# A decoder layer on one core: dense steps between the state-space matmuls, and the embedding's result staged in the tiles of later operands

## The chip, the cores and the metric

The kernel runs on 1 core of one Trainium2 chip. The metric is the device time of one execution in microseconds (us); lower is better. Several executions are timed and the median is quoted; one execution more is profiled.

## What is computed

One layer of a decoder trunk in float32, with 1024 tokens of 1024 channels. Four token mixers of 256 channels each run on the same stream, and a gated sum of their outputs goes through one projection. A squared-ReLU MLP and a gated embedding follow. Cut to what matters here:

```python
proj = h @ w_in[i]
(s5_u, fq, fk, fv, ff, rw, sq, sk, sv, gates) = _split(proj, IN_SPLIT_SIZES)
y_s5 = _s5_mixer(s5_u, ...)          # diagonal complex state space, 16 groups of 16 channels
y_fox, y_rwkv, y_sb = ...            # forgetting attention, RWKV-7, stick-breaking attention
merged = sum(jax.nn.sigmoid(gates[:, :, n]) * (branches[n] @ w_branch[i, n])
             for n in range(N_BRANCHES))
h = _layer_norm(DEEPNORM_ALPHA * h + merged @ w_out[i], ln1_g[i], ln1_b[i])
ffn = jnp.square(jax.nn.relu(h @ mlp_w1[i])) @ mlp_w2[i]
ple = jax.nn.sigmoid(h @ ple_gate_w[i]) * (p[i] @ ple_w[i])
h = _layer_norm(DEEPNORM_ALPHA * h + ffn + ple, ln2_g[i], ln2_b[i])
```

Inside `_s5_mixer` a scan over the tokens gives the states, `y` is the output of the states and of the input, and then `y = gelu(y)` and `y * sigmoid(y @ glu_w + glu_b)`.

## The kernel before, in words

Nearly all dense products are made of three matmuls of 128x512 each, because both operands are split into a high and a low part (high by high, high by low, low by high). The function `dense` makes such a product; it yields after each step of 128 rows of the contraction, that is after three matmuls. In the first part of the kernel, the projections, weights are `wh` and `wl` (or `vh` and `vl` for the branches' up-projections) and the operands are the tiles `t` (the input x) and `y` (a mixer's output). Weights come in as `wr`, ScalarE casts them to `wh` and VectorE makes `wl`.

The mixers are written as generators, run by a planner (the class `Driver`). It keeps a clock of its own, made of estimated costs. `run(fill, until)` goes on with the generator that is due and has the best priority; when none is due it takes one step from `fill`, the dense projections. A generator that says `yield None` is due again 0.2 us of planned time later, so that one dense step is taken before it goes on; a number sets another time. The order that comes out is binding for TensorE, VectorE and ScalarE. The DMA queues of SP and POOL are ordered by the tile scheduler. Since every instruction of VectorE, ScalarE and the queues is issued by a wrapper (`Timed`), most of them stand at line 280; matmuls stand at line 327 and transposes at 332.

The state-space mixer has two generators. `s5_tables` makes matrices from the parameters: eight pairs of matmuls of `Gm` by `bd` go into a tile `lo`, and `Gm` is transposed in 16 pieces, four to a PSUM tile, which ScalarE copies to `GT`. Then `s5` runs twice, over 8 groups of channels each: 16 matmuls of `GT` by `U` give the inputs of the states, VectorE rotates them, scans over the tokens and rotates back (`X`), and an output loop makes for each of 8 groups one matmul of `Tg` by `U` and two of `Hm` by `X`. A GELU follows. When both passes are done, `gw` by `yt` makes the gate, in 128x512 float32. The result `ynat` is stored to `scr_Y` in DRAM, and loaded back as `wr`, to be split to the operand `y` of the up-projection. The next mixer, the stick-breaking attention, loads `raw` and `st` (keys, queries and values), multiplies `KH`, `KL` by `QS`, makes `R` and `W` on ScalarE, scans on VectorE, and transposes `W`.

The MLP is computed with a scheme that combines blocks of weights and operands before multiplying (seven products take the place of eight). Before it, `ple_half` makes the embedding's product, eight tiles for each half of the tokens; each is evicted from PSUM by ScalarE with a factor of 0.5 and stored to `scr_B`. Once the pool `sp` is open, the eviction takes a tile from `sn()`: ten buffers with a live count that the planner watches, shared with the intermediate results of the MLP's operand combinations. The operands of the first four products lie in other tiles; those of the last ones (`T3`, `B22`, `T4`) are [128, 1024] tiles with the tag `sx`, 12 buffers. Weight combinations are made partly by DMAs of POOL that accumulate (`wr<-wl`, `wl<-wr`), and `wp` are the split weight pairs.

Lines that the change touches: 1331 (`lo`), 1343 (transposes of `Gm`), 1424 (output loop of `s5`) and 2086 to 2092 (`ple_half`).

Of the kernel before, what the change touches and what calls it, by code (L numbers as in the profile page):

```python
# [9 lines left out]
F32 = mybir.dt.float32  # L10
# [6 lines left out]
P = 128  # L17
# [299 lines left out]
def body(ctx, tc, I, O, dbg=None):  # L317
# [25 lines left out]
    def nm(s):  # L343
        uid[0] += 1
        return f"{s}_{uid[0]}"
# [924 lines left out]
    def s5_tables(pool):  # L1270
        pw, fr, fi = s5v["pw"], s5v["fr"], s5v["fi"]

        def small(shape, name):
            return pool.tile(shape, F32, tag="s2k", name=nm(name), bufs=4)
        bc_in = small([P, 4, 8, 16], "bcin")
        SY.dma_start(out=bc_in, in_=I["s5_bc"])
        br, bi, cr, ci = (bc_in[:, i] for i in range(4))
        dsb = small([P, 256], "dsb")
        G.dma_start(out=dsb, in_=I["s5_d"].partition_broadcast(P))
        zz = small([112, 256], "zz")  # L1280
        G.memset(zz, 0.0)
        SY.dma_start(out=SCR["L"][128:240], in_=zz)

        def t1k(shape=(P, 8, 8, 16)):
            return pool.tile(list(shape), F32, tag="t1k", name=nm("t1k"), bufs=2)
        E = pool.tile([P, 2, P, 8], F32, tag="E", name="E", bufs=1)
        V.memset(E[:, 0, 0, :], 1.0)
        V.memset(E[:, 1, 0, :], 0.0)

        def grow(k):  # L1290
            n = 1 << k
            bcs = [x.unsqueeze(1).to_broadcast([P, n, 8]) for x in s5v["steps"][k]]
            cmul(E[:, 0, n:2 * n, :], E[:, 1, n:2 * n, :], E[:, 0, 0:n, :], E[:, 1, 0:n, :], bcs[0], bcs[1],
                 lambda: t1k((P, 64, 8))[:, :n, :])

        def b16(a):
            return a.unsqueeze(2).to_broadcast([P, 8, 16])
        bb = pool.tile([P, 2, 8, 16], F32, tag="bb", name="bb", bufs=1)

        def t128():  # L1300
            return pool.tile([P, 8, 16], F32, tag="t128", name=nm("t128"), bufs=4)
        for k in range(5):
            grow(k)
            if k % 2:
                yield 0.1
        cmul(bb[:, 0], bb[:, 1], b16(fr), b16(fi), br, bi, t128)
        nci = pool.tile([P, 8, 16], F32, tag="nci", name="nci", bufs=1)
        ts(nci, ci, -1.0, ALU.mult)
        bd = pool.tile([P, 2, 8, 2, 16], F32, tag="bd", name="bd", bufs=1)
        G.memset(bd, 0.0)  # L1310
        for e in range(2):
            es = slice(e * 64, e * 64 + 64)
            for i, w in ((0, cr), (1, nci)):
                A.copy(bd[es, i, :, e, :], w[es])
        yield 0.1
        pwp = pw.rearrange("p i j a -> p i a j")
        Gm = pool.tile([P, 2, 8, 8, 16], F32, tag="a", name="Gm", bufs=1)
        Hm = pool.tile([P, 2, 8, 8, 16], F32, tag="Hm", name="Hm", bufs=1)

        def bj(a):  # L1320
            return a.unsqueeze(3).to_broadcast([P, 8, 8, 16])

        def bh(a):
            return a.unsqueeze(2).to_broadcast([P, 8, 8, 16])
        prev = [pwp[:, i, :, 7::-1] for i in range(2)]
        pnx = [pwp[:, i, :, 1:9] for i in range(2)]
        cmul(Gm[:, 0], Gm[:, 1], bj(prev[0]), bj(prev[1]), bh(bb[:, 0]), bh(bb[:, 1]), t1k)
        yield 0.1
        lo = px()
        for pr in range(8):  # L1330
            for i in range(2):
                T.matmul(lo[:, pr * 32:pr * 32 + 32], lhsT=Gm[:, i, pr].rearrange("p s h -> p (s h)"),
                         rhs=bd[:, i, pr].rearrange("p e h -> p (e h)"), start=i == 0, stop=i == 1)
        Ls = small([P, 256], "Ls")
        tt(Ls.rearrange("p (g h) -> p g h", h=16), dsb.rearrange("p (g h) -> p g h", h=16),
           cc("eye7").unsqueeze(1).to_broadcast([P, 16, 16]), ALU.mult)
        tt(Ls, Ls, lo[:, 0:256], ALU.add)
        SY.dma_start(out=SCR["L"][0:128], in_=Ls)
        GT = pool.tile([P, 2, 8, P], F32, tag="GT", name="GT", bufs=1)
        for i in range(2):  # L1340
            for p4 in range(2):
                o = px()
                for j in range(4):
                    T.transpose(o[:, j * P:(j + 1) * P], Gm[:, i, p4 * 4 + j].rearrange("p s h -> p (s h)"), ident)
                A.copy(GT[:, i, p4 * 4:p4 * 4 + 4, :].rearrange("p a b -> p (a b)"), o)
        U = pool.tile([P, 16, P], F32, tag="a", name="U", bufs=1)
        for s in range(8):
            SY.dma_start(out=U[s * 16:(s + 1) * 16], in_=SCR["u"].rearrange("(g h) s c -> s h g c", h=16)[s])
        a1, a2 = t1k(), t1k()
        tt(a1, bj(pnx[0]), bh(cr), ALU.mult)  # L1350
        tt(a2, bj(pnx[1]), bh(ci), ALU.mult)
        tt(Hm[:, 0], a1, a2, ALU.subtract)
        yield 0.1
        a1, a2 = t1k(), t1k()
        tt(a1, bj(pnx[0]), bh(nci), ALU.mult)
        tt(a2, bj(pnx[1]), bh(cr), ALU.mult)
        tt(Hm[:, 1], a1, a2, ALU.subtract)
        Tg = pool.tile([P, 16, 8, 16], F32, tag="Tg", name="Tg", bufs=1)
        for s in range(0, 8, 2):
            Tz = small([P, 2, 256], "Tz")  # L1360
            for i in range(2):
                SY.dma_start(out=Tz[:, i, :], in_=SCR["L"][(7 - s - i) * 16:(7 - s - i) * 16 + 128])
            A.copy(Tg[:, :, s:s + 2, :], Tz.rearrange("p s (g h) -> p g s h", h=16))
        for k in range(5, 7):
            grow(k)
            yield 0.1
        yield from s5(pool, GT, Tg.rearrange("p g s h -> p g (s h)"), Hm.rearrange("p i a s h -> p i a (s h)"),
                      E.rearrange("p i j a -> p i a j"), U)

    def s5(pool, GT_, Tg_, Hm_, E_, U_):  # L1370
# [9 lines left out]
        for p4 in range(2):  # L1380
# [37 lines left out]
            for g4 in range(2):  # L1418
                o = px()
                for j in range(4):  # L1420
                    g = j * 2 + g4
                    pr, es = g // 2, slice((g % 2) * 64, (g % 2) * 64 + 64)
                    os_ = o[:, j * P:(j + 1) * P]
                    T.matmul(os_, lhsT=Tg[:, g], rhs=U[:, g, :], start=True, stop=False)
                    for i in range(2):
                        T.matmul(os_, lhsT=Hm[es, i, pr], rhs=X[es, i, pr, :], start=False, stop=i == 1)
                w = pool.tile([P, 512], F32, tag="s2k", name=nm("gl"), bufs=4)
                A.activation(out=w, in_=o, func=AF.Square)
                V.tensor_scalar(out=w, in0=w, scalar1=0.044715, scalar2=1.0, op0=ALU.mult, op1=ALU.add)
                tt(w, o, w, ALU.mult)  # L1430
                A.activation(out=w, in_=w, func=AF.Tanh, scale=math.sqrt(2.0 / math.pi))
                V.scalar_tensor_tensor(out=Ye[:, g4], in0=w.rearrange("p (a b) -> p a b", b=P), scalar=1.0,
                                       in1=o.rearrange("p (a b) -> p a b", b=P), op0=ALU.add, op1=ALU.mult)
# [87 lines left out]
    def sp():  # L1521
        return late["sp"]
# [272 lines left out]
    def sn():  # L1795
        live["sn"] += 1
        return sp().tile([P, 512], F32, tag="sn", name=nm("sn"), bufs=NSN)

    def drop(what):
        live[what] -= 1  # L1800
# [268 lines left out]
    def ple_half(h):  # L2069
        for dt_ in range(8):  # L2070
            k = 2 + dt_ // 2
            while (h, k) not in fed_units:
                yield "wait"
            o = pmm()
            for kt in range(2):
                xa, xb = fed_units[h, kt]
                ks = slice(dt_ % 2 * 256 + kt * P, dt_ % 2 * 256 + kt * P + P)
                a, b = (x[:, ks] for x in fed_units[h, k])
                T.matmul(o, lhsT=a, rhs=xa, start=kt == 0, stop=False)
                T.matmul(o, lhsT=a, rhs=xb, start=False, stop=False)  # L2080
                T.matmul(o, lhsT=b, rhs=xa, start=False, stop=kt == 1)
                yield
            if dt_ % 2:
                used_units.add((h, k))
            here = "sp" in late
            t = sn() if here else tpool.tile([P, 512], F32, tag="th", name=nm("pb"), bufs=2)
            A.activation(out=t, in_=o, func=AF.Copy, scale=0.5)
            SY.dma_start(out=SCR["B"][dt_][:, h * 512:(h + 1) * 512], in_=t)
            if here:
                drop("sn")  # L2090

    def open_sp():
        while tdone[0] < 8:
# [158 lines left out]
```

## Time and profile before

| what | value |
|---|---|
| median of 3 runs | 1868.21 us |
| lowest and highest | 1867.77 and 1874.67 us |
| profiled execution, its own time | 1875.13 us |
| its span, first to last instruction | 1873.3 us |
| mean granted clock of TensorE | 0.983 |
| busy share of TensorE, VectorE, ScalarE, GpSimd | 97%, 66%, 38%, 11% |
| mean DMA rate | 147 GB/s |

The span is cut to stretches by views of the trace, which give for each engine its busy time and for TensorE the granted clock (1.00 is 2.4 GHz, 0.50 is 1.2 GHz). A timeline gives start and length of each instruction or run of like instructions and, in brackets, the idle time before it and what ended that. Starts of successive matmuls are a better measure of their rate than lengths, since matmuls overlap.

### The profile page before, as it was taken

The page shows a single profiled execution, that of the slowest core. Times are in us where ns is not written, and L with a number is a line of the kernel's source. Part 1 is how long each engine was busy: PE and PEld are TensorE (multiplying, and loading weights), DVE is VectorE, ACT ScalarE, POOL GpSimd, SP SyncE. Part 2 cuts the span into 40 slices and gives each one's busy share as a digit, 9 for nine tenths or more (in the row PEclk, how much of TensorE's full clock was granted, in tenths as well). Part 3 has the DMA queues.
Part 4 walks back from the last instruction along what each step waited for, and adds up shares of the span by engine and source line. Part 5 has one row for each costly group of instructions (what it writes and reads, how often), then busy time and mean ns, then how long its engine had stood idle before and what let it go on. Part 6 is the DMA issues. An engine that isn't in the chain of part 4 may idle for free. (4 is left out here: it accounts for less than half of the span.)

```text
span 1873.3 us, 27588 instructions
## 1 busy us (share of the span) xinstructions
PE 1816.4 (97%) x9651; PEld 1479.0 (79%) x9651; DVE 1237.8 (66%) x2596; ACT 714.3 (38%) x1412; POOL 206.9 (11%) x279
## 2 busy tenths in 40 slices
PE   8999999998999999999999998999999999999998
PEld 6877777777788877777877886788888887888876
DVE  7675855616876765688867667666656565866574
ACT  5443343215554212555544125343333343433230
POOL 0331111100000000000000001111121111111000
PEclk9999999999999988999999999999999999999999
DMA  7334223124422411412155118898989898988441
GB/s 254 108 123 112 76 81 95 63 69 139 146 90 78 104 38 50 137 54 67 44 197 160 62 57 234 239 254 223 255 235 251 212 268 256 284 212 229 127 147 48
DMA packets 178012, 275.27 MB, mean 147 GB/s; under 512 B 37824, under 2 KB 59616, under 8 KB 177744
## 3 DMA queue, kind: packets, MB, share of 16 engines
q1 hardware_dynamic: 155552, 226.31, 37.3%
q0 software_dynamic: 22320, 47.18, 12.8%
q8 instruction: 76, 1.25, 0.3%
q14 instruction: 64, 0.52, 0.1%
HBM read 199.76 MB, written 56.89 MB: 137 GB/s over the span
## 5 line engine op out<-in xcount | busy, mean ns | idle before, releaser
L327 PE MATMUL mm<-t,wh 128*128 128x512 f32 x1600 | 514.3, 403 | 3.8 <-ACT th L280 1.9
L327 PEld LDWEIGHTS mm<-t,wh 128*128 128x128 f32 x1600 | 293.8, 190 | 66.5 <-issue 2.4
L327 PE MATMUL mm<-t,wl 128*128 128x512 f32 x800 | 314.9, 394 | 0.0
L327 PE MATMUL x<-t,wp 128*128 128x512 f32 x1152 | 270.8, 394 | 14.1 <-DVE wp L280 6.8
L327 PEld LDWEIGHTS x<-t,wp 128*128 128x128 f32 x1152 | 217.7, 190 | 64.3 <-DVE wp L280 9.9
L327 PE MATMUL x<-sx,wp 128*128 128x512 f32 x768 | 179.6, 389 | 0.2 <-DVE wp L280 0.2
L327 PEld LDWEIGHTS mm<-t,wl 128*128 128x128 f32 x800 | 151.8, 190 | 33.4
L327 PEld LDWEIGHTS x<-sx,wp 128*128 128x128 f32 x768 | 144.1, 188 | 30.5 <-DVE wp L280 0.7
L280 ACT CAST wh<-wr 128x512 fp32r<-128x512 f32 (+1 forms) x125 | 74.5, 596 | 123.1 <-PE mm L327 90.7
L280 DVE TENSOR_TENSOR wp<-wr,wp 128x512 fp32r<-128x512 f32 x96 | 65.8, 687 | 77.2 <-ACT wp L280 77.2
L280 ACT CAST wp<-wr 128x512 fp32r<-128x512 f32 x96 | 59.1, 620 | 147.8 <-DMA wr<-wl 69.3
L280 POOL TENSOR_TENSOR wl<-wr,wh 128x512 fp32r<-128x512 f32 x50 | 67.7, 1353 | 280.6 <-ACT wh L280 280.4
L327 PE MATMUL mm<-t,wp 128*128 128x512 f32 x384 | 90.6, 392 | 0.0
L327 PE MATMUL mm<-sx,wp 128*128 128x512 f32 x384 | 89.6, 389 | 0.0
L327 PE MATMUL mm<-wo,t 128*128 128x512 f32 x384 | 89.0, 391 | 0.0
L327 PEld LDWEIGHTS mm<-t,wp 128*128 128x128 f32 x384 | 72.6, 189 | 15.6 <-DVE wp L280 0.4
L327 PEld LDWEIGHTS mm<-sx,wp 128*128 128x128 f32 x384 | 72.1, 188 | 14.9
L327 PEld LDWEIGHTS mm<-wo,t 128*128 128x128 f32 x384 | 71.6, 188 | 14.5
L280 DVE TENSOR_TENSOR wl<-wr,wh 128x512 fp32r<-128x512 f32 (+1 forms) x75 | 47.3, 633 | 40.4 <-ACT wh L280 39.5
L280 DVE TENSOR_TENSOR wp<-wl,wp 128x512 fp32r<-128x512 f32 x64 | 43.7, 687 | 42.5 <-ACT wp L280 42.5
L280 DVE TENSOR_TENSOR wp<-wh,wp 128x512 fp32r<-128x512 f32 x64 | 43.9, 689 | 33.7 <-ACT wp L280 33.7
L280 ACT CAST wp<-wl 128x512 fp32r<-128x512 f32 x64 | 39.3, 620 | 50.0 <-DMA wl<-wr 16.5
(380 smaller groups left out, 3199.4 us busy)
## 6 DMA issues: line engine op xcount, KB each, us to landing
wr<-in_w_in_dram SPq DMA_DIRECT2D x110, 256.0 KB
scr_H<-sn SPq DMA_DIRECT2D x100, 256.0 KB
wr<-in_mlp_w_dram SPq DMA_DIRECT2D x84, 256.0 KB
sn<-scr_H SPq DMA_DIRECT2D x84, 256.0 KB
wh<-in_mlp_w_dram SPq DMA_DIRECT2D x56, 256.0 KB
wl<-in_mlp_w_dram SPq DMA_DIRECT2D x56, 256.0 KB
wr<-wl POOLq DMA_DIRECT2D x32, 256.0 KB, 6.5
wl<-wr POOLq DMA_DIRECT2D x32, 256.0 KB, 4.7
```

What stands on the lines that cost most here:

```text
L280: r = f(*a, **kw)
L327: return nc.tensor.matmul(out, lhsT=lhsT, rhs=rhs, **kw)
```

## The change

Three `yield None` are put into the state-space mixer: after each of the 8 pairs of `lo`, after each of the 4 groups of transposes, and after each of the 16 groups of the output loop (8 in each pass). Between these the planner now takes a dense step. And the evictions of `ple_half` take the first half of an `sx` tile once the pool is open, in place of a tile from `sn()`; the live count no longer holds them.

```diff
             for i in range(2):
                 T.matmul(lo[:, pr * 32:pr * 32 + 32], lhsT=Gm[:, i, pr].rearrange("p s h -> p (s h)"),
                          rhs=bd[:, i, pr].rearrange("p e h -> p (e h)"), start=i == 0, stop=i == 1)
+            yield None
...
                 for j in range(4):
                     T.transpose(o[:, j * P:(j + 1) * P], Gm[:, i, p4 * 4 + j].rearrange("p s h -> p (s h)"), ident)
                 A.copy(GT[:, i, p4 * 4:p4 * 4 + 4, :].rearrange("p a b -> p (a b)"), o)
+                yield None
...
                     T.matmul(os_, lhsT=Tg[:, g], rhs=U[:, g, :], start=True, stop=False)
                     for i in range(2):
                         T.matmul(os_, lhsT=Hm[es, i, pr], rhs=X[es, i, pr, :], start=False, stop=i == 1)
+                    yield None
...
             here = "sp" in late
-            t = sn() if here else tpool.tile([P, 512], F32, tag="th", name=nm("pb"), bufs=2)
+            t = (sp().tile([P, 1024], F32, tag="sx", name=nm("pb"), bufs=12)[:, 0:512] if here else
+                 tpool.tile([P, 512], F32, tag="th", name=nm("pb"), bufs=2))
             A.activation(out=t, in_=o, func=AF.Copy, scale=0.5)
             SY.dma_start(out=SCR["B"][dt_][:, h * 512:(h + 1) * 512], in_=t)
-            if here:
-                drop("sn")
```

TensorE, output loop of the state-space mixer, before (second half of the first pass; `x_` is the output's PSUM tile, `mm_` that of a dense product):

```order
L327 MATMUL x_7490<-U,Tg 128x128
L327 MATMUL x_7490<-X_7310,Hm 128x128 x2
L327 MATMUL x_7490<-U,Tg 128x128
L327 MATMUL x_7490<-X_7310,Hm 128x128 x2
L327 MATMUL x_7490<-U,Tg 128x128
L327 MATMUL x_7490<-X_7310,Hm 128x128 x2
L327 MATMUL x_7490<-U,Tg 128x128
L327 MATMUL x_7490<-X_7310,Hm 128x128 x2
L327 MATMUL mm_7464<-t_111,wh_7317 128x512
L327 MATMUL mm_7464<-t_110,wh_7317 128x512
L327 MATMUL mm_7464<-t_111,wl_7318 128x512
```

The same place after the change:

```order
L327 MATMUL x_7342<-U,Tg 128x128
L327 MATMUL x_7342<-X_7174,Hm 128x128 x2
L327 MATMUL mm_7308<-t_115,wh_7178 128x512
L327 MATMUL mm_7308<-t_114,wh_7178 128x512
L327 MATMUL mm_7308<-t_115,wl_7179 128x512
L327 MATMUL x_7342<-U,Tg 128x128
L327 MATMUL x_7342<-X_7174,Hm 128x128 x2
L327 MATMUL mm_7308<-t_117,wh_7178 128x512
L327 MATMUL mm_7308<-t_116,wh_7178 128x512
L327 MATMUL mm_7308<-t_117,wl_7179 128x512
```

Each group of three small matmuls now has one dense step behind it.

TensorE, the first use of the state-space result before the change (`y_7733` and `y_7734` are the high and low part of it, `vh_7803` the weight); between the gate's matmuls and the row mm_7904 stand 90 dense matmuls, two groups of transposes of `st` and the eight matmuls of `KH` and `KL`:

```order
L327 MATMUL x_7888<-KH_7682,QS_7681 128x384
L327 MATMUL x_7888<-KL_7683,QS_7681 128x384
L327 MATMUL mm_7822<-t_121,wh_7702 128x512
L327 MATMUL mm_7822<-t_120,wh_7702 128x512
L327 MATMUL mm_7822<-t_121,wl_7703 128x512
L327 MATMUL mm_7904<-y_7733,vh_7803 128x512
L327 MATMUL mm_7904<-y_7734,vh_7803 128x512
L327 MATMUL mm_7904<-y_7733,vl_7804 128x512
```

The same first use after the change (`y_7794`, `y_7795`, `vh_7824`); between the gate's matmuls and the row mm_7830 stand 21 dense matmuls and one group of transposes:

```order
L327 MATMUL mm_7701<-t_121,wl_7639 128x512
L332 MATMUL x_7802<-cst,st_7773 128x64 x4
L327 MATMUL mm_7830<-y_7794,vh_7824 128x512
L327 MATMUL mm_7830<-y_7795,vh_7824 128x512
L327 MATMUL mm_7830<-y_7794,vl_7825 128x512
L332 MATMUL x_7834<-cst,st_7775 128x64 x4
L327 MATMUL mm_7830<-y_7814,vh_7824 128x512
```

The first use has moved ahead of the second group of transposes and of the `KH`, `QS` block, and 69 dense matmuls that stood between the gate and it now stand ahead of the gate.

ScalarE, evictions of the embedding's product at the start of the MLP, before (`sn_` are the staged tiles; in brackets the semaphores waited for, DMAHW being those of SP's transfers):

```order
L280 CAST wp_11684<-wr_11608 128x512 [waits DMAHW7_49]
L280 ACTIVATE sn_11694<-mm_11671 128x512 [waits DMAHW6_49,PE_49,Activation_49]
L280 ACTIVATE sn_11704<-mm_11697 128x512 [waits DMAHW0_49,PE_49,Activation_49]
L280 CAST wp_11711<-wr_11610 128x512 [waits DMAHW1_49]
L280 ACTIVATE sn_11721<-mm_11707 128x512 [waits DMAHW0_49,PE_49,Activation_49]
```

After (`pb_` are the staged tiles):

```order
L280 CAST wp_11684<-wr_11608 128x512 [waits DMAHW7_49]
L280 ACTIVATE pb_11694<-mm_11671 128x512 [waits PE_49]
L280 ACTIVATE pb_11704<-mm_11697 128x512 [waits PE_49]
L280 CAST wp_11711<-wr_11610 128x512 [waits DMAHW1_49]
L280 ACTIVATE pb_11717<-mm_11707 128x512 [waits PE_49]
```

The evictions stand where they stood, and no longer wait for a store.

## Rows read from the trace of the kernel before

**Rows 1.** Windows: busy time by engine, granted clock, DMA share, GB/s, around the three blocks.

```profile
625.00:637.00 12.00, 12.00 (x65) 11.11 (x64) 7.60 (x11) 3.17 (x6) 0.00 (x0) 0.72 0.21 44
680.00:700.00 20.00, 20.00 (x70) 15.21 (x72) 7.48 (x13) 3.26 (x6) 0.00 (x0) 0.57 0.13 35
712.00:732.00 20.00, 18.60 (x66) 14.22 (x65) 10.22 (x16) 2.51 (x5) 0.00 (x0) 0.66 0.22 64
```

**Rows 2.** Timeline of TensorE, first block: start, length, instruction, shapes, count.

```profile
630.29 3.65 PE L332 MATMUL x<-cst,Gm 128*128 128x128 f32 x16
633.60 1.20 PE L327 MATMUL mm<-t,wh 128*128 128x512 f32 x2
...
636.16 0.62 PE L327 MATMUL mm<-t,wh 128*128 128x512 f32 x2
...
636.85 0.62 PE L327 MATMUL mm<-t,wh 128*128 128x512 f32 x2
```

**Rows 3.** Timeline of TensorE, output loop of the first pass.

```profile
680.28 0.78 PE L327 MATMUL x<-U,Tg 128*128 128x128 f32 x2
...
693.38 1.22 PE L327 MATMUL mm<-t,wh 128*128 128x512 f32 x2
...
698.10 0.62 PE L327 MATMUL mm<-t,wh 128*128 128x512 f32 x2
```

**Rows 4.** Timeline of TensorE, output loop of the second pass.

```profile
715.06 0.49 PE L327 MATMUL x<-U,Tg 128*128 128x128 f32 x2
...
717.17 0.49 PE L327 MATMUL x<-U,Tg 128*128 128x128 f32 x2
...
725.99 1.22 PE L327 MATMUL mm<-t,wh 128*128 128x512 f32 x2
...
732.10 0.62 PE L327 MATMUL mm<-t,wh 128*128 128x512 f32 x2
```

**Rows 5.** Windows of dense matmuls (mm tiles) alone, RWKV part: TensorE busy, clock, DMA.

```profile
200.00:205.00 5.00, 2.73 (x11) 1.00 0.18 52
235.00:240.00 5.00, 0.65 (x3) 1.00 0.44 105
```

**Rows 6.** Timeline of TensorE, from the gate's matmuls to the W transposes.

```profile
745.04 7.03 PE L327 MATMUL x<-yt,gw 128*128 128x512 f32 x16
...
775.27 0.62 PE L327 MATMUL mm<-y,vh 128*128 128x512 f32 x2
...
781.27 1.06 PE L332 MATMUL x<-cst,W 128*128 128x128 f32 x8 [0.24 <-DVE W L280]
...
784.71 0.98 PE L332 MATMUL x<-cst,W 128*128 128x128 f32 x7 [0.98 <-DVE W L280]
...
800.03 0.84 PE L332 MATMUL x<-cst,W 128*128 128x128 f32 x6 [0.17 <-DVE W L280]
```

**Rows 7.** Timeline of SP's queue, load of the up-projection's weight.

```profile
766.32 0.38 SPq L280 DMA_DIRECT2D wr<-in_w_branch_dram  x1
```

**Rows 8.** Timeline of ScalarE, weight cast and first R.

```profile
770.37 0.40 ACT L280 CAST vh<-wr 128x256 fp32r<-128x256 f32 x1
...
775.20 0.60 ACT L280 ACTIVATE R<-x 128x512 f32<-128x512 f32 x1
```

**Rows 9.** Waits at the start of the MLP, 1105 to 1200 us.

```profile
ACT sn L280 <- DMA scr_B<-sn: 8.2, 2, 4.7
...
DVE sn L280 <- DMA scr_B<-sn: 5.4, 4, 2.5
```

**Rows 10.** Timeline of ScalarE, cast of the second weight pair.

```profile
1150.24 0.62 ACT L280 CAST wp<-wr 128x512 fp32r<-128x512 f32 x1 [0.88 <-DMA wr<-wl]
```

**Rows 11.** Timeline of TensorE, start of the MLP.

```profile
1155.22 0.73 PE L327 MATMUL x<-t,wp 128*128 128x512 f32 x2 [1.01 <-ACT wp L280]
1159.21 4.63 PE L327 MATMUL x<-t,wp 128*128 128x512 f32 x10 [3.26 <-DVE wp L280]
1163.64 2.65 PE L327 MATMUL mm<-t,wp 128*128 128x512 f32 x8
```

## The prediction, made before the changed kernel had run

> **What bounds the kernel now.** The page gives TensorE 97% of the span, so a microsecond counts only if TensorE idles less, or does its work at the higher clock. I read the granted clock first, in stretches of 5 us and then around the three places that the change edits; then TensorE's timeline there, what waits around the start of the MLP, and last the instruction order of both kernels.
>
> The clock falls at each place where the state-space work stands as one block: mean 0.72, 0.57 and 0.66 of full speed in the three stretches [rows 1]. A dense step (three matmuls) starts 0.69 us after the step before it at full clock (last two of [rows 2]), so 0.227 us a matmul. A group of the output loop takes 13.10 / 7 = 1.87 us in the second stretch [rows 3] and 2.11 / 2 = 1.06 us where the clock still stood, early in the third [rows 4]. Two levels, 2.4 and 1.2 GHz, explain both.
>
> **The change part by part.**
>
> *What the lower clock costs.* First stretch: 16 transposes take 633.60 - 630.29 = 3.31 us, half of it lost (1.65), and two dense steps 2.56 instead of 1.37, so 1.2; the tail of the bd,Gm block about 0.4: 3.2 us [rows 2]. Second: 7 groups lose 7 x 0.81 = 5.7, and four dense steps take 4.72 instead of 2.75: 7.7 us [rows 3]. Third: five groups take 8.82 instead of 5.30, and five dense steps 6.11 instead of 3.43: 6.2 us [rows 4]. Sum 17.1 us.
>
> *Does putting dense steps between bring it back?* Nothing in these stretches shows that, so I bound it: 0 from the blocks as they are, 17.1 if the clock stays. The nearest rows are the RWKV part, where small matmuls and dense steps alternate already: dense matmuls hold 2.73 of 5 us in one stretch and 0.65 of 5 in another, and the clock is 1.00 in both [rows 5]. With a dense step of 0.69 beside a group of 1.06 the share is 0.39, between those two. I take 17.1.
>
> *What the yields pull forward.* 28 yields, one dense step each. Part of these steps stood there before; counted in the two orders, 387 dense matmuls instead of 318 run between the first block and the gate's matmuls (yt,gw), so 69 x 0.227 = 15.7 us of dense work come earlier. That work isn't added, it is taken from behind. So yt,gw starts at 745.0 - 17.1 + 15.7 = 743.6 [rows 6], only 1.4 us earlier, and call that time G.
>
> *What is late next.* Behind yt,gw the planner had 90 dense matmuls, two groups of transposes and the KH,QS block before the first use of the S5 result (mm<-y,vh at 775.27, G + 30.2 [rows 6]); now it has 21 and one group of transposes. So TensorE comes to that matmul at G + 7.0 + 4.8 + 0.4 = G + 12.2, and waits for the weight half vh. Its load is issued on SP behind the six raw loads, which follow the stores and loads of S5's own result, at 766.32 = G + 21.3 [rows 7]; none of this hangs on TensorE's clock. The cast stood at G + 25.3 behind other casts [rows 8] and now stands ahead of them. Bounds: G + 23 and G + 26; I take G + 24.4, nearer the row. New idle time: about 12 us. Queued behind that matmul are the second transposes and KH,QS, and ScalarE's Vh cast and R wait for these.
>
> After such a wait the clock is low: after 3.26 us of idle ten matmuls took 4.43 us instead of 2.27 [rows 11], so 2.2 us more. Five dense steps of y at 3.4, transposes 0.4: KH,QS begins at G + 30.4, R about 0.6 later, G + 31.0, where it stood at G + 30.2 [rows 8]. From R the chain over VectorE's scan to the first and second W transposes is 6.1 and 9.5 us [rows 6, 8], so the second come at G + 40.5. From there to the six W transposes at 800.03 it was 15.3 us with 42 dense matmuls; now 24 stand there, 4.1 us less: G + 51.7 = 795.3. There both orders agree again, and the new one has done 3 dense matmuls more. **State-space part: 800.0 - 795.3 + 0.7 = 5.4 us gained**, not 17.1. Ends: 2.5 (vh at G + 26, longer at half clock) and 8 (vh at G + 23, clock back at once).
>
> *The staged result.* ScalarE waited 8.2 us and VectorE 5.4 us for stores of these tiles to drain [rows 9], because the evictions shared ten buffers with the operands' intermediate tiles. Twelve evictions now take the twelve sx tiles, whose first operand use is later, so both engines come earlier to the intermediates. Cost of the wait that replaces it: an sx cast that must wait for its store, over ten us later; I cost it at nothing, covered by that time (if not, each costs a DMA's rest, a few us at most). TensorE gains less: its second pair of weights hangs on an accumulating load, which releases ScalarE's cast at 1150.24 [rows 10], and nothing before 1150.9 moves. The idle spans of 1.01 and 3.26 us behind it, on late casts, and the half clock of 2.2 us after the latter [rows 11] can go: 6.5 at most, and no more than the 5.4 of VectorE. Against that, the idle spans before 1150.9 merge into one longer one that may cost the clock there, 2.2. Ends 0 and 5.4; I take 3.0, the middle with part of the clock paid again.
>
> Sum: 5.4 + 3.0 = 8.4 us. On the profiled execution, 1875.1, that gives 1866.7; that one stands 6.9 us above the median of the runs, so against 1868.2 it is **1859.8 us**. No change that a measurement can tell is one under 0.5%, 9.3 us; the forecast is just inside it.
>
> **A rule weighed.** Eight W transposes among dense steps began at 781.27 and took 1.06 us, 0.13 each [rows 6], against 0.21 each in the first stretch [rows 2]: between dense steps they ran at the full clock. The Trainium skill, "TensorE: Matmul & The Clock Gate", Part 4: PE-mode transpose, says that a transpose does not count as busy for the clock in the way that a matmul does. By that rule the four transpose groups would keep the lower clock; that is the third rival.
>
> **The rivals.**
> - *The clock doesn't come back* (slower). A group is still longer than the dense step beside it. For: the clock fell in the third stretch after two groups at full speed, in the one begun at 717.17 [rows 4]. Against: [rows 5]. If all of it stays at half speed, 16 groups cost 16 x 0.81, 28 dense steps 28 x 0.6, and the first blocks some 5 us more: 35 us, and since what follows G is a chain, all of it shows. With half of that, 17.5 - 8.4 = 9 us slower, 1877. It decides from 8.4 us of lost clock on. Chance 0.11.
> - *The new wait doesn't bite* (much faster): S5's result is there when TensorE comes. The whole 17.1 and the 3.0 are gained, 1848. For: in [rows 8] vh stands behind casts which it doesn't need. Against: the stores and loads of S5's result take until G + 21 on SP [rows 7]. Partly true gives some 1854. Chance 0.15.
> - *Transposes hold the clock down*: 1.65 and four dense steps at 0.6 are not given back, 4.1 less, 1864. Chance 0.04.
> - *The second part gives nothing*, because the accumulating loads set the pace of the MLP's start: 5.4 us alone, 1862.8. Chance 0.12.
>
> **How the numbers follow.** The forecast keeps 0.58, with a spread of 4 to 13 us by the ends above; 0.30 of it lies over 9.3 us. Faster: 0.30 + 0.15 = 0.45. Slower: 0.10 of the first rival. Same: the rest, 0.45. The range: 1850 takes in most of the second rival's part gains, 1869 the ends of all but the first rival; about 0.2 lies outside.
>
> **What would show it.** Right: granted clock over 0.95 from 625 to 735; groups every 1.75 us with a dense step in each; yt,gw at about 743.6; one wait of 10 to 13 us before mm<-y,vh and a low clock after it; the six W transposes at 795; no ScalarE or VectorE wait on scr_B stores; the MLP's second weight pair with no 3 us idle after it. The prediction is wrong if the clock stays under 0.8 between the groups, if yt,gw comes later than 749, or if the wait at y is under 5 us.

## The result, and the profile after

The changed kernel is slower: its median is 1888.33 us (1882.29 to 1895.53, six runs) beside 1870.18 us before (1867.06 to 1874.67, six runs); ratio 1.0093, 95% interval 1.0066 to 1.0121. The forecast was 1859.8 us, with a range of 1850 to 1869. The profiled execution took 1893.17 us (span 1891.4, mean clock 0.977), 18.0 us more than that of before.

The three places are the first block (the pairs of `lo` and the transposes of `Gm`) and the two output loops. First the granted clock around them, for which [rows 1] stand before (columns: stretch, its length, TensorE's busy time and instructions, granted clock, DMA share, GB/s):

```profile
625.00:640.00 15.00, 15.00 (x90) 1.00 0.30 90
681.00:705.00 24.00, 24.00 (x70) 0.51 0.09 28
725.00:750.00 25.00, 25.00 (x73) 0.52 0.07 23
```

The first block, now with dense steps between, runs at 1.00. The output loops are at half clock almost from end to end, and they are longer than before, since the dense steps in them are slow too. TensorE's timeline of the first of them, which answers to [rows 3]:

```profile
679.87 0.46 PE L327 MATMUL x<-X,Hm 64*128 64x128 f32 x2 [1.37 <-DVE X L280]
...
681.19 0.39 PE L327 MATMUL x<-U,Tg 128*128 128x128 f32 x2
...
684.11 0.63 PE L327 MATMUL x<-U,Tg 128*128 128x128 f32 x2
...
687.26 0.63 PE L327 MATMUL x<-U,Tg 128*128 128x128 f32 x2
```

After 1.37 us of idle time for X the first group and dense step are at full clock (the next group starts at 681.19), then the clock falls: from 684.11 to 687.26 one group and one dense step take 3.15 us, and would take 1.75. The tail, for [rows 6]:

```profile
763.88 7.03 PE L327 MATMUL x<-yt,gw 128*128 128x512 f32 x16
...
788.92 1.22 PE L327 MATMUL mm<-y,vh 128*128 128x512 f32 x2 [12.85 <-ACT vh L280]
...
816.38 0.85 PE L332 MATMUL x<-cst,W 128*128 128x128 f32 x6 [0.16 <-DVE W L280]
...
829.93 0.69 PE L332 MATMUL x<-cst,st 64*128 64x64 f32 x4 [3.84 <-DMA st<-scr_qk]
```

yt,gw starts 18.8 us later than before, the first use of the S5 result waits 12.85 us for vh, and a load of `st` holds TensorE once more at 829.93. The start of the MLP, for [rows 11]:

```profile
1148.54 11.17 PE L327 MATMUL mm<-t,t 128*128 128x512 f32 x48
...
1174.16 8.41 PE L327 MATMUL x<-t,wp 128*128 128x512 f32 x24 [3.57 <-ACT wp L280]
1182.40 5.96 PE L327 MATMUL mm<-t,wp 128*128 128x512 f32 x24
```

Where there were four idle spans (1.10, 1.72, 1.01 and 3.26 us, the last two in [rows 11]) there is one now, of 3.57 us. The waits of ScalarE and VectorE on stores to scr_B [rows 9] are gone; what is left there is POOL's:

```profile
POOL wr L280 <- DMA scr_B<-pb: 6.5, 1, 6.5
```

The 18 us between the two profiled executions, place by place (start of the row in either):

| place | before | after | later by |
|---|---|---|---|
| yt,gw | 745.04 | 763.88 | 18.8 |
| six W transposes, where the orders meet | 800.03 | 816.38 | 16.4 |
| MLP's first product, mm<-t,t (timelines) | 1125.81 | 1148.54 | 22.7 |
| first block of four weights done, mm<-t,wp | 1163.64 | 1182.40 | 18.8 |
| end of the span | 1873.3 | 1891.4 | 18.1 |

Of the first 18.8 us, 15.7 are the 69 dense matmuls pulled forward. The three places together gave back no clock: the sum of (1 - clock) over the time from 620 us to yt,gw, which is what a busy TensorE loses to the lower clock, is 18.8 us before and 23.9 us after, 5.1 us more. Against that, the first block began 2.4 us earlier in this execution (623.84, before 626.25). From the W transposes to the MLP 6.4 us are added; there stand 3.84 us of idle time for `st` and low clock behind it. The staging gains 4.0 us.

A note for all that follows: executions of one and the same kernel differ by up to 10 us and more, also within one chip. The sum of (1 - clock) over the time from 620 to 760 us shows a part of the reason: it is 18.8 us in the profiled execution of before, which was one of its longer ones, and 13.7 us in the run with only the staging changed, whose state-space part has the same order. So traces are read here for the mechanism, and times from the medians and ratios, always against the kernel before on the same chip.

### The profile page after: what moved, and what is told of

Same layout as the page of the kernel before. It is cut to its first block, busy times and chain, and to the rows that moved or that the text cites. A ratio compares the mean times of both kernels' runs of the same rounds, so it can differ in the third digit from the quotient of the medians.

```text
span 1891.4 us, 27608 instructions
## 1 busy us (share of the span) xinstructions
PE 1822.8 (96%) x9651; PEld 1483.9 (78%) x9651; DVE 1237.3 (65%) x2596; ACT 714.1 (38%) x1412; POOL 206.5 (11%) x279
## 5 line engine op out<-in xcount | busy, mean ns | idle before, releaser
L327 PE MATMUL mm<-t,wh 128*128 128x512 f32 x1600 | 520.2, 407 | 1.2 <-DVE th L280 1.2
L327 PE MATMUL mm<-y,vh 128*128 128x512 f32 x176 | 58.8, 417 | 12.9 <-ACT vh L280 12.9
```

Of the source, the lines that this page charges most:

```text
L327: return nc.tensor.matmul(out, lhsT=lhsT, rhs=rhs, **kw)
```

## The experiments

Two theories stood after the result. Theory 1: the interleaving works in the first block but not in the output loops, and the dense work pulled forward is missing later, as cover for the way of the S5 result. Rival: the loops are a side issue, any dense work pulled forward is paid for in the tail.

### One part alone, three times, and two together

First block only (the first two hunks of the change):

```diff
                          rhs=bd[:, i, pr].rearrange("p e h -> p (e h)"), start=i == 0, stop=i == 1)
+            yield None
...
                 A.copy(GT[:, i, p4 * 4:p4 * 4 + 4, :].rearrange("p a b -> p (a b)"), o)
+                yield None
```

> Only the yields of the first block (pairs of lo, groups of transposes); output loops and the embedding's staging as before. Theory 1 (the two places behave differently: between bd,Gm pairs and transposes dense steps hold the clock, in the output loop they don't): granted clock 1.00 through the first block, the output loops low as before the change (6 and 9 us at half clock each), 3.2 us of clock come back and the first use of the S5 result waits 0 to 3 us; 1 to 5 us faster than before. Rival (any dense work pulled ahead of the gate is paid back in the tail's wait): clock the same as theory 1, but a wait of 5 us or more at the first use, and 0 to 4 us slower.

Measured: 1873.93 us, ratio 1.0053 (1.0032 to 1.0074): 7.7 us slower by the medians, where theory 1 had 1 to 5 us faster. The clock did hold in the first block, and in a place that no theory had named a new wait appeared:

```profile
625.00:640.00 15.00, 15.00 (x92) 1.00 0.26 82
```

```profile
715.32 1.22 PE L327 MATMUL mm<-t,wh 128*128 128x512 f32 x2 [3.84 <-DVE th L280]
...
749.79 7.03 PE L327 MATMUL x<-yt,gw 128*128 128x512 f32 x16
...
775.30 0.73 PE L327 MATMUL mm<-y,vh 128*128 128x512 f32 x2 [0.43 <-ACT vh L280]
```

The first use of the S5 result waits only 0.43 us, as expected, for 69 dense matmuls stand behind the gate. But the dense stream ahead of the second loop has moved by 21 matmuls against the state-space chain, so that a product's eviction (th) now falls behind the chain's work on VectorE: there the last piece of X starts at 713.98 and the eviction behind it at 714.59, and TensorE has waited 3.84 us for the PSUM tile. After that idle time the second loop is at half clock from its first group to its end, though no idle time stands within it. So theory 1's account of the clock holds here, and its time doesn't: it had no term for this wait. Nor is the loss accounted for in full: the first use of the S5 result comes at 775.30, as in the profiled execution of before (775.27), but 5.2 us later than with only the staging changed (770.13), where less clock was lost. VectorE's timeline there:

```profile
713.98 0.69 DVE L280 TENSOR_TENSOR X<-tq,tq 128x508 f32<-128x508 f32 x1
714.59 0.68 DVE L280 SCALAR_TENSOR_TENSOR th<-th,mm 128x512 f32<-128x512 f32 x1
```

Output loops only (the third hunk):

```diff
                         T.matmul(os_, lhsT=Hm[es, i, pr], rhs=X[es, i, pr, :], start=False, stop=i == 1)
+                    yield None
```

> Only the yields of the output loops. Theory 1: the clock stays at half through both interleaved loops, 16 dense steps cost 0.6 us more each, so yt,gw comes some 6 us later than the dense steps pulled ahead explain; 48 dense matmuls after the gate, so the wait at the first use of the S5 result is 5 to 8 us, not 12.9; 10 to 18 us slower than before. Rival (the loss of the whole change came from the tail alone, the number of dense matmuls behind the gate): at most 5 us slower.

Measured: 1895.08 us, ratio 1.016 (1.0118 to 1.0201), slower than the whole change. Theory 1's mechanism stands (0.53 and 0.50 in the loops, a wait of 6.25 us for vh), but the price, 29 us by the medians, lies far above its 10 to 18; a wait for th of 3.83 us ahead of the second loop and one of 4.02 us for `st` weren't in it.

```profile
677.00:702.00 25.00, 25.00 (x74) 0.53 0.09 27
720.00:750.00 30.00, 29.64 (x82) 0.50 0.11 36
```

Staging only (the hunk in `ple_half`):

```diff
-            t = sn() if here else tpool.tile([P, 512], F32, tag="th", name=nm("pb"), bufs=2)
+            t = (sp().tile([P, 1024], F32, tag="sx", name=nm("pb"), bufs=12)[:, 0:512] if here else
+                 tpool.tile([P, 512], F32, tag="th", name=nm("pb"), bufs=2))
...
-            if here:
-                drop("sn")
```

> Only the embedding's result staged in sx tiles. Theory: no ScalarE or VectorE wait on stores of these tiles, one wait of 3 to 4 us before the second weight pair instead of four smaller ones, 3 to 5 us faster than before. Rival (accumulating loads set the pace): within 1 us of before.

Measured: 1863.1 us, ratio 0.9983 (0.9961 to 1.0004), 3.2 us by the medians, an interval that just takes in no change. In the trace the stretch is plain:

```profile
1119.18 11.26 PE L327 MATMUL mm<-t,t 128*128 128x512 f32 x48
...
1144.92 5.28 PE L327 MATMUL x<-t,wp 128*128 128x512 f32 x14 [3.60 <-ACT wp L280]
...
1153.16 5.97 PE L327 MATMUL mm<-t,wp 128*128 128x512 f32 x24
```

From the MLP's first product to mm<-t,wp it takes 33.98 us; before it was 37.83 (1125.81 to 1163.64), in the run with the first block alone 38.26. So the gain is 3.9 us here, and one idle span of 3.60 us stands where theory put it.

First block and staging together (both diffs above, no new edit):

> The yields of the first block and the staging, no yields in the output loops. If the parts add: the sum of the two runs with one part each, 4 to 9 us faster than before. Rival (the MLP's gain is eaten by the loads at its end): no better than the better one of the two.

Measured: 1871.21 us, ratio 1.0027 (1.0008 to 1.0047). The two parts' ratios give 1.0053 x 0.9983 = 1.0036: they add, though the expected sign was wrong, since the first block alone is a loss.

### Why the clock falls in the loops

Behind the first few matmuls of each output loop TensorE is idle while VectorE finishes X. In the kernel before it was so in both:

```profile
679.90 0.46 PE L327 MATMUL x<-X,Hm 64*128 64x128 f32 x2 [1.38 <-DVE X L280]
...
714.67 0.46 PE L327 MATMUL x<-X,Hm 64*128 64x128 f32 x2 [1.40 <-DVE X L280]
```

Theory A: that idle time makes the clock fall. Theory B: the loop's own small matmuls do. The pause that a planner step asks for was made longer, so that three dense steps more come ahead of the loop and X is there:

```diff
             Ye = Y.rearrange("p (a e) c -> p e a c", e=2)
-            yield 0.1
+            yield 2.6
```

In the changed kernel:

> The whole change, with the pause before each output loop 2.6 us of planned time instead of 0.1, so that a few dense steps more stand ahead of the loop and X is there when its first matmul comes: takes away the idle time of 1.4 to 2.1 us at the loop's start. Theory A (that idle time makes the clock fall and the thin dense share only fails to lift it): the clock stays 1.00 through both interleaved loops, yt,gw at most 69 dense matmuls later than in the fast case. Theory B (the loop's own small matmuls, 1.06 us beside 0.69 us of dense, let the clock fall): idle time gone, and yet 0.50 from some 3 us into the loop to its end. More dense matmuls stand ahead of the gate in either case, none behind it, so the wait for vh is 15 to 20 us; the time is 15 to 35 us above before.

Measured: 1874.79 us, ratio 1.0062 (1.0037 to 1.0086), 7.6 us above before by the medians, where 15 to 35 were expected. The clock:

```profile
680.00:684.00 4.00, 3.96 (x12) 0.63 0.41 131
685.00:698.00 13.00, 13.00 (x67) 1.00 0.05 11
710.00:730.00 20.00, 20.00 (x101) 1.00 0.00 1
```

```profile
680.04 0.74 PE L327 MATMUL mm<-t,wh 128*128 128x512 f32 x2 [2.52 <-DVE th L280]
...
716.96 0.38 PE L327 MATMUL x<-U,Tg 128*128 128x128 f32 x2
...
718.74 0.38 PE L327 MATMUL x<-U,Tg 128*128 128x128 f32 x2
...
747.35 7.03 PE L327 MATMUL x<-yt,gw 128*128 128x512 f32 x16
...
771.71 1.22 PE L327 MATMUL mm<-y,vh 128*128 128x512 f32 x2 [16.95 <-ACT vh L280]
```

The second loop has no idle time ahead, and a group with its dense step takes 718.74 - 716.96 = 1.78 us in place of 3.15. The first one has a wait of 2.52 us for th, three dense steps before the loop; the clock falls after it and is back after the first group. So one dense step after each group goes with a held clock where no idle time stands in the loop, and theory B falls. The time is still above before; 16.95 us are spent in the wait for vh, since no dense matmul is left behind the gate.

In the kernel before, with the output loops as blocks, that is without yields in them:

> The kernel before the change with the same longer pause: output loops as blocks, without the idle time ahead. Theory A: the clock holds through the block of 8.5 us, or falls late in it, and 5 to 10 us come back in the stretches; Theory B: it falls some 3 to 5 us into the block, as it did in the second pass of the kernel before, and at most 3 us come back in each. Some 60 dense matmuls less the pulled ones stand behind the gate, so the wait for vh stays under 2 us.

Measured: 1860.75 us, ratio 0.9966 (0.9941 to 0.9991): faster.

```profile
676.00:686.00 10.00, 10.00 (x57) 1.00 0.21 66
707.00:717.00 10.00, 10.00 (x56) 1.00 0.22 64
```

```profile
676.81 0.38 PE L327 MATMUL x<-U,Tg 128*128 128x128 f32 x2
...
684.10 0.49 PE L327 MATMUL x<-U,Tg 128*128 128x128 f32 x2
...
705.11 0.50 PE L327 MATMUL mm<-t,wl 128*128 128x512 f32 x1 [2.81 <-DVE wl L280]
...
707.51 0.38 PE L327 MATMUL x<-U,Tg 128*128 128x128 f32 x2
```

Both blocks run at full clock from end to end, seven groups in 684.10 - 676.81 = 7.29 us, 1.04 us each, with no dense step between them. The wait of 2.81 us at 705.11, three dense steps ahead of the second block, did not bring the clock down here. One thing these runs don't separate: the longer pause takes the idle time out of the loop by putting dense steps ahead of it.

Two dense steps for each group, in the changed kernel:

```diff
                         T.matmul(os_, lhsT=Hm[es, i, pr], rhs=X[es, i, pr, :], start=False, stop=i == 1)
                     yield None
+                    yield None
```

> The whole change with two dense steps after each group of the output loop: dense matmuls 1.38 of 2.44 us, instead of 0.69 of 1.75. Idle time at the loop's start stays. Theory B (share of dense work): the clock stays up or comes back within the loop. Theory A (idle time, then stuck): it falls as in the changed kernel and stays at 0.50 to the loop's end. No dense matmuls stand between the gate and the S5 result's first use, so that wait is 16 to 19 us; the time is 10 to 35 us above before.

Measured: 1885.65 us, ratio 1.0127 (1.0067 to 1.0187).

```profile
682.00:700.00 18.00, 17.95 (x88) 1.00 0.20 66
721.00:726.00 5.00, 5.00 (x19) 0.66 0.02 3
726.00:740.00 14.00, 14.00 (x70) 1.00 0.00 0
```

```profile
681.58 0.46 PE L327 MATMUL x<-X,Hm 64*128 64x128 f32 x2 [1.38 <-DVE X L280]
...
720.44 0.50 PE L327 MATMUL mm<-t,wl 128*128 128x512 f32 x1 [3.39 <-DVE wl L280]
...
780.23 1.22 PE L327 MATMUL mm<-y,vh 128*128 128x512 f32 x2 [16.46 <-ACT vh L280]
```

With 1.38 us of idle time at its start the first loop holds 1.00, where the changed kernel with one dense step fell after the same wait; in the second the clock falls after 3.39 us of idle time and is back from 725.7 on, within the loop. So the second dense step helps after idle time, as theory B said, though it isn't needed without; this rests on one profiled execution. Both can't be had here: 16.46 us of wait for vh are the price.

The kernel before with a shorter pause:

```diff
-            yield 0.1
+            yield 1.2
```

> The kernel before with a pause of 1.2 us instead of 2.6: one dense step more ahead of the first loop, so some 0.7 us of its 1.4 us of idle time stay. If the length of the idle time decides (theory A): the clock falls later in the block than before, or not, and 2 to 6 us come back. If only the place in time decides: as before, within 2 us.

Measured: 1866.59 us, ratio 0.9985 (0.9971 to 1.0).

```profile
677.00:689.00 12.00, 12.00 (x42) 0.52 0.18 55
711.00:724.00 13.00, 13.00 (x42) 0.53 0.29 87
```

```profile
675.83 0.46 PE L327 MATMUL x<-X,Hm 64*128 64x128 f32 x2 [0.74 <-DVE X L280]
...
709.12 0.46 PE L327 MATMUL x<-X,Hm 64*128 64x128 f32 x2 [0.82 <-DVE X L280]
```

Half of the idle time is left, 0.74 and 0.82 us, and in both blocks the clock falls some 2 us after it. By the medians the time is 1.3 us under before, not the 2 to 6 us expected if the length decided. So within what was tried the length of the idle time doesn't matter, against this form of theory A, but its presence does: 0.74 us in a block without dense steps go with a fall, and none goes with a held clock.

### What the two readings give together

Blocks with the longer pause, and the staging (the diffs of those two runs):

> The output loops as blocks with the longer pause ahead (as in the run with that alone), and the embedding's result staged in sx tiles; none of the yields. If both gains stand and add: clock 1.00 in both output loops again, the stretch from the MLP's first product to the first block of four weights (mm<-t,wp) 34 us instead of 38, and 8 to 11 us faster than before, the best of all kernels. Rival (the held clock of the one profile was luck): one of the loops at 0.50 again and at most 5 us faster.

Measured: 1859.7 us (1853.43 to 1868.26), beside 1867.85 for before; ratio 0.9948 (0.9927 to 0.9968). It has the lowest ratio of all, though its interval overlaps that of the longer pause alone. The ratios of its parts give 0.9966 x 0.9983 = 0.9949. In its profiled execution, of 1868.26 us, the clock fell after the wait of 2.81 us ahead of the second block, so the rival's sign was there in part. It was back by the second group, in a block without dense steps:

```profile
676.00:686.00 10.00, 10.00 (x57) 1.00 0.19 66
706.00:709.00 3.00, 3.00 (x9) 0.50 0.50 151
709.00:718.00 9.00, 9.00 (x51) 0.98 0.13 29
```

The same with the yields of the first block:

> The same with the yields of the first block. Theory: the first block's clock is held, worth 0 to 3 us, but 84 dense matmuls less stand behind the first block, so the wait for vh comes back at some 5 us (63 dense matmuls between the gate and the first use of the S5 result, 14 us, against vh at 24.5): 3 to 8 us slower than the kernel without these yields. Rival: no more than 1 us apart.

Measured: 1872.96 us, ratio 1.003 (1.0012 to 1.0048): 13 us above the kernel without them, more than the 3 to 8 expected. The wait for vh is 5.11 us, as worked out; two waits for th came with it. The second output loop, without dense steps and without idle time in it, runs at 1.00.

```profile
718.00:727.00 9.00, 9.00 (x52) 1.00 0.03 4
```

```profile
679.81 0.74 PE L327 MATMUL mm<-t,wh 128*128 128x512 f32 x2 [2.52 <-DVE th L280]
...
711.68 1.22 PE L327 MATMUL mm<-t,wh 128*128 128x512 f32 x2 [5.78 <-DVE th L280]
...
767.33 1.22 PE L327 MATMUL mm<-y,vh 128*128 128x512 f32 x2 [5.11 <-ACT vh L280]
```

Between this kernel, the one with the pause and the whole change (1874.79 us) and the fastest one only yields differ, and in all three the output loops hold the clock for most of their length; the sum of (1 - clock) from 620 to 760 us is 5.1, 1.9 and 1.7 us (23.9 in the changed kernel). The yields cost 13 us and some 16 us there (the second from 7.6 above and 8.2 below before, each on its own chip). Most of that is waits: from 620 to 860 us TensorE is idle for 19.2 and 25.8 us, beside 9.4 in the kernel without yields.

### The tail, over all runs

| kernel | dense matmuls from the gate to the first use of the S5 result | vh used at, after the gate's start | wait there |
|---|---|---|---|
| before | 90 | 30.2 us | none |
| first block only | 69 | 25.5 us | 0.43 |
| first block, pause, staging | 51 | 24.3 us | 5.11 |
| output loops only | 48 | 24.8 us | 6.25 |
| whole change | 21 | 25.0 us | 12.85 |
| whole change and pause | 0 | 24.4 us | 16.95 |
| whole change, two dense steps | 0 | 28.2 us | 16.46 |
| first block and staging | 69 | 25.9 us | 0.77 |
| pause; pause and staging | 72 | 26.0 us | none |
| short pause | 84 | 28.5 us | none |
| staging only | 90 | 30.2 us | none |

Where TensorE waits, the result is there 24.3 to 25.9 us after the gate's start, with the clock high or low ahead of it; only with two dense steps it is 28.2 us, and there the gate itself stood idle for 2.35 us, until its operand yt was loaded. In 24.5 us TensorE can do (24.5 - 7) / 0.227 = 77 dense matmuls beside the gate's own, an estimate that leaves out the small matmuls in between. The planner's dense stream is one list, and in the order of every kernel here the same 408 dense matmuls stand between the start of the first block and that use; each that is pulled ahead of the gate is missing behind it. By this estimate the kernel before had 90 - 77 = 13 to spare, and the change took 69.

## Why the prediction was wrong

- **"I take 17.1", the clock that comes back: this step failed.** By the sum of (1 - clock) it measured -5.1: the first block gave back 3.4 (worked out: 3.2), but the two loops lost 23.9 us in place of 15.3, 8.6 more. The rows that I chose as nearest [rows 5] have no idle time ahead, and the loops do, 1.4 us for X, which no term of the prediction has. The runs with the longer pause show that without this idle time one dense step a group goes with a held clock, and that even blocks without dense work hold it. What holds a fallen clock down through a loop is not settled: after waits of 2.52 and 2.81 us with three dense steps behind them it came back within the block, after 3.84 us with one dense step behind, in the run with the first block only, it didn't.
- The first rival, that the clock doesn't come back, is what happened, and its price was near: 9 us slower with half of the stretch at half clock, 35 - 8.4 = 26.6 with all of it, 18 measured with nearly all of both loops and the first block held. Its reason, that a group is longer than the dense step beside it, held only in part: a second dense step helps after idle time, but not even the first is needed without.
- yt,gw at 743.6 became 763.88, nearly all of it from that step: 17.1 not given back and 5.1 more lost, less the 2.4 by which this execution was ahead. The count of 69 dense matmuls was right.
- The new wait was right: about 12 us forecast, 12.85 measured. R came at G + 31.6, where the working had G + 31.0, and the six W transposes at G + 52.5 (816.38 - 763.88), where it had G + 51.7.
- "There both orders agree again" missed what it means for loads: TensorE's order is the same, but at the transposes of `st` it waits 3.84 us for their load, with low clock behind; 6.4 us were added there that no term held. The run with the first block only, with 0.43 us of wait for vh, has no such wait (0.48 us); those with 5 us or more for vh all have one of 3.6 to 4.0. Why the load comes late was not tried by itself.
- The state-space part is likely to be a loss without the clock's fall, too, which no run shows by itself. With the longer pause and the clock held, the changed kernel was 7.6 us above before, though it has the staging's gain; of that the pause itself, which takes the last 21 dense matmuls from behind the gate, can account for 21 x 0.227 = 4.8 us, an estimate. My working had 5.4 gained.
- The second part was right in mechanism and size: 3.0 forecast, 4.0 and 3.9 measured in the traces, 3.2 by the medians, with one idle span of 3.6 us in place of four.
- The third rival, that transposes hold the clock down, is out: in six profiled executions with dense steps between them (the changed kernel among them) the first block was at 1.00. The Trainium skill, "TensorE: Matmul & The Clock Gate", Part 4: PE-mode transpose, says that a transpose doesn't count as busy in the same way. No effect of that is seen where dense steps stand between. Without dense steps between, the block lost clock in three of six profiled executions, 1.7 to 3.4 us, and none in the other three, so that the gain there is 0 to 3.4 us rather than 3.2.

## What to carry to other kernels

Before dense work is put between small matmuls to hold the clock, look at what stands just ahead of the block: here the clock fell in every block with a wait of about a microsecond in it, and moving three dense steps ahead of it, to cover that wait, gave more than putting sixteen into it. Filler is a stock: what is pulled forward is missing where the next latency chain needs it, so count the matmuls that a later wait can spare before spending them. And a shift of one stream against another can change which PSUM eviction stands behind which chain, and so make waits where the diff touches nothing.

## What was not expected of the hardware

- Output loops as blocks of small float32 matmuls, about 8 us long and nothing between, ran at a granted clock of 1.00 in four cases without idle time in the block (both of the kernel before with the longer pause, the first with pause and staging, the second with the first block's yields added), and fell to 0.50 in every one with 0.74 to 1.41 us of it. A clock that was already low at the block's start came back within it in two cases and stayed low to its end in two (the second loops with the first block's yields and no pause).
- Once low, the clock stayed at 0.50 through a stretch of 24 us in which a dense step of three 128x512 matmuls followed every group of three small ones (681 to 705, mean 0.51), though TensorE was never idle in it; with the same steps and no idle time it stayed at 1.00 (710 to 730, with the longer pause).
- The same instruction order lost 18.8 us of clock between 620 and 760 us in one execution and 13.7 us in another; one profiled execution of a kernel is a poor measure of what its clock costs.
